# Narrower expert products, an output projection ordered by tile, and a fixed order at the experts' end, in a two-layer hybrid backbone on one core

## The chip, the core and the metric

The kernel runs on one core of a Trainium2 chip. Five engines work beside each other, each with its own instruction stream: TensorE (PE for products, PEld for the loads of its stationary operand), VectorE (DVE), ScalarE (ACT), GpSimd (POOL) and SyncE (SP). A transfer is issued in an engine's stream and carried out by 16 DMA engines. The metric is the device time of one execution in microseconds (us), the median over several runs.

## The reference

The reference is two layers over 256 latent and 256 context tokens of width 1024. Each layer adds a token mixer and then a mixture of experts to its residual stream, both with scales, shifts and gates that come from a conditioning vector.

```
xl = xl + g1_x * (ox @ w_out)                       # output projection
hx = modulate(xl, norm_g[l, 1], sh2_x, sc2_x)       # second norm
pg = softmax(h @ wg + bg); pg_top, g_sel = top_k(pg, 1)
le_g = (h @ we + be) of group g_sel; pe_top, e_sel = top_k(softmax(le_g), 2)
for e in range(16):                                 # D = 1024, d_expert = 512
    y = (silu(h @ w1[e]) * (h @ w3[e])) @ w2[e]
    out = out + combine[:, e:e + 1] * y
xl = xl + g2_x * out
```

Layer 0 mixes with a recurrence (RWKV-7) and a short convolution and carries all 512 tokens on. Layer 1 mixes with differential attention and neighbourhood attention, and only its 256 latent tokens go on to the output. All data is 32-bit.

## The kernel before, in words

**Helpers.** Nearly all products go through `mm` (L214), transposes through `flip` (L219), weight loads through `wload` (L202, on SP's queue). `split` (L224) writes a high part on ACT and the remainder on DVE; a projection is the sum of three products of such parts (`out_mm`: two by L214, the third by L407). `bcast` (L296) reads a modulation row from DRAM into all 128 partitions, on POOL's queue. A planner sets the order of each engine's instructions by dependencies and costs, except where instructions carry a token: those of one token keep the order in which they are written (`inorder`). With `in_line` set all products and transposes carry one.

**Output projection of layer 0** (`out_proj`). The product `wo` has 4 tiles of 128 tokens and two halves h of 512 columns; a tile's half takes 8 input chunks k, 24 products of 512 columns. When a tile's half is complete, DVE multiplies by the gate (`wt`, L435, needs the gate row `g`) and adds to the stream (`x`, L436). `token_norm` follows: sum of squares (L490), scaling with `sc` (L491; `sc` itself is built at L488), and after h = 1 the root and the shift (`hfs`, L502). The **router part** then stands in the same call: per half of the width 4 transposes `rT`, a copy to `hT` on ACT (L514), 4 products `rl` of 20 columns. In h = 1 the order is a table: tiles 0 and 1 whole, then tiles 2 and 3 interleaved by halves of k.

**Experts of layer 0** (`all0`). Each of 16 experts has 96 slots. Its token rows are fetched and transposed (`xt`, copied to `XE`), multiplied by w1 and w3 (`hidden`, four steps q), gated (`middle`), transposed (`gT`) and multiplied by w2 (`down`). In `hidden` the 96 slots are two sets: slots 0 to 63 as stationary operands 64 columns wide, two products side by side (`h`, 32 products of 512 columns per expert), and slots 64 to 95 as operands 32 wide, four side by side (`hc`, 32 products). `down` does the same with `y`, 16 products of each width, for experts 0 to 13; the last two use one operand of 96. The program's order on PE for expert e is fixed: step 0 of e+1, `gT` of e, step 1 of e+1, `down` of e, `xt`, step 2, `xt`, step 3. `middle` stands in the order's gaps on ACT and DVE: `gs` (L893, L894), `gg` (L901, L902, L905). Weights stream in on SP's queue, 12 loads of 512 KB per expert (6.29 MB); 96 token rows of 4 KB come in and as many result rows go out on POOL's (0.79 MB together).

**The experts' end.** The last expert results are not sent through DRAM but placed by products `sc` with 0/1 matrices (`last_two`, two halves per tile, out of one PSUM tag). `fetched` adds the other experts' rows per tile (L940 to L943). Then `tt` (L1083) and `x` (L1084) finish a tile, `norm1_begin` and `norm1_end` normalise it for layer 1, `norm1_turn` transposes it (`nT`), and `proj1` multiplies by `od_w_in`, whose first weights it loads and splits itself (`whi`, `wlo`). After the experts no token is set, so the planner may move this splitting into their end.

Of the kernel before, what the change touches and what calls it, by code (L numbers as in the profile page):

```python
# [11 lines left out]
F32 = mybir.dt.float32  # L12
F32R = mybir.dt.float32r
# [8 lines left out]
P = 128  # L22
# [113 lines left out]
def tile_kernel(ctx: ExitStack, tc: tile.TileContext, I, out, stage=99, dbg=None):  # L136
# [155 lines left out]

    def bcast(pool, tag, l, i, v, bufs=1, n=D, off=0, dst=None):

        t = pool.tile([P, n], F32, tag=tag, name=tag, bufs=bufs) if dst is None else dst
        nc.gpsimd.dma_start(t, bass.AP(tensor=adaD.tensor, offset=adaD.offset + (l * 2 + i) * 6144 + v * D + off,  # L296
                                       ap=[[0, P], [1, n]]))
        return t
# [66 lines left out]

    def norm1_turn(x, khi, klo):

        xn = norm1["xn"]
        xn[0] = cp.tile([P, 2, D], F32, tag="x4", name="xn")
        for t in (2, 3, 0, 1):  # L370
            c = slice(t * 128, t * 128 + 128)
            if t < 2:
                norm1_begin(x, t, lambda inst: None)
                norm1_end(t, lambda inst: None)
            for g in range(2):
                tp = ps("nT", ("ga", "gT")[g])
                for k in range(4):
                    flip(tp[:, k * 128:(k + 1) * 128], token_tile(xn, t)[:, (4 * g + k) * 128:(4 * g + k + 1) * 128],
                         ident)
                split(tp.rearrange("p (k t) -> p k t", k=4), khi[g][:, :, c], klo[g][:, :, c])  # L380
            if t == 3:
                yield xn
        yield

# [13 lines left out]
    def out_gate(l, pool, h):  # L398

        return [bcast(pool, f"g1{i}", l, i, 2, n=512, off=h * 512) for i in range(2 if l == 0 else 1)]  # L400

# [9 lines left out]
    def out_proj(l, Wo, tiles, pool, oT, x1, gate1, done, late, order, tags=("wo",), begun=None):  # L411

        n = len(tiles)
        for h in range(2):
            hs = slice(h * 512, h * 512 + 512)
            g1 = gate1 if h == 0 else out_gate(l, pool, h)
            old, ws = begun if begun and h == 0 else (None, {})
# [9 lines left out]
            for k, a in [(k, a) for k in ks for a in range(n)] if h == 0 else order:  # L429
                out_mm(accs[a], oT, a, k, ws[k], seen[a] == 0, seen[a] == 7)  # L430
                seen[a] += 1
                if seen[a] == 8:
                    t = tiles[a]
                    tt = pool.tile([P, 512], F32, tag="wt", name="wt", bufs=2)
                    inorder(V.tensor_tensor(tt, accs[a], g1[1 if t < 2 else 0], op=ALU.mult), "sums")  # L435
                    (G if h == 0 and a % 2 else V).tensor_tensor(token_tile(x1, t)[:, hs], tt, token_tile(x1, t)[:, hs],  # L436
                                                                 op=ALU.add)
                    if h:
                        done(a, h)
            if h == 0:  # L440
                for a in range(n):
                    done(a, h)


# [5 lines left out]
    def moe(l, tiles, cap, ng, x1, pm, pn, hhi=None, hlo=None):  # L450
# [15 lines left out]
        if l == 0:  # L466
# [7 lines left out]
        ngb = pn.tile([P, D], F32, tag="hT", name="ngb")  # L474
        nc.gpsimd.dma_start(ngb, bass.AP(tensor=I["norm_g"].tensor,
                                         offset=I["norm_g"].offset + (2 * l + 1) * D, ap=[[0, P], [1, D]]))
        sc2 = [bcast(pn, f"sc2{i}", l, i, 4) for i in range(nconds)]
        sh2 = [bcast(pn, f"sh2{i}", l, i, 3) for i in range(nconds)]
        hold = {}

        def token_norm(a, h):
# [22 lines left out]
            if f"h2_{l}" in dbg:  # L504
                nc.sync.dma_start(dbg[f"h2_{l}"][a * P:(a + 1) * P, :], hf)
            acc2 = ps("rl", "rl")
            hT2 = pn.tile([P, D], F32, tag="hT", name="hT")
            for g in range(2):
                acc = ps("rT", "rT")
                for k in range(4):  # L510
                    flip(acc[:, k * 128:(k + 1) * 128],
                                        hf[:, (4 * g + k) * 128:(4 * g + k + 1) * 128], ident)
                hT = hT2[:, g * 512:(g + 1) * 512]
                inorder(act(hT, acc, AF.Copy), "moe")  # L514
                for k in range(4):
                    mm(acc2[:, 0:20], hT[:, k * 128:(k + 1) * 128], wge[:, 4 * g + k, :],
                       start=(g == 0 and k == 0), stop=(g == 1 and k == 3))
            V.tensor_tensor(lg[:, a, :], acc2[:, 0:20], rt[:, 160:180], op=ALU.add)
            if l == 1:
                split(hf, hhi[a], hlo[a])  # L520

# [111 lines left out]
        def experts(pe, ysb, rest, spare=None, next_norm=None):  # L633
# [178 lines left out]
            def all0(rest):  # L812
# [41 lines left out]
                def load(n):  # L854

                    while len(loaded) < min(n, len(stream)):
                        e, u = stream[len(loaded)]
                        q = u % 4
                        if u < 8:
                            w = wload(I[("moe_w1", "moe_w3")[u // 4]][l, e, q * 256:(q + 1) * 256, :], 2, 512)  # L860
                        else:
# [12 lines left out]
                def hidden(e, q):  # L874
# [36 lines left out]
                def down(e, gT):  # L911
# [86 lines left out]
                for e in range(16):  # L998
# [67 lines left out]
                in_line[0] = False  # L1066
                token[0] = None
                slots[:] = base
                turn[0] = 0
# [4 lines left out]
                def last_two(a, t):  # L1074

                    for h in range(2):
                        acc = ps("sc", "h")
                        for i in range(2):
# [680 lines left out]
    with tc.tile_pool(name="pO", bufs=1) as pO:  # L1759

        x1 = [cp.tile([P, 2, D], F32, tag="x", name="x1", bufs=2) for _ in range(2)]
        for i, nm in enumerate(("ctx", "x")):
            nc.gpsimd.dma_start(x1[i], I[nm][0].rearrange("(t p) d -> p t d", p=P))
        gate1 = out_gate(0, pO, 0)
        token[0] = "tail"
# [17 lines left out]
    with tc.tile_pool(name="pe0", bufs=1) as pe:  # L1783
# [7 lines left out]

        experts(pe, ysb, rest, spare, (norm1_scales, norm1_begin, norm1_end))
    es_m.close()
# [33 lines left out]
    with ExitStack() as es:  # L1827
# [3 lines left out]
        dv = pP.tile([P, 4, 512], F32, tag="y", name="dv")  # L1831
        kt = [[pP.tile([P, 4, 512], F32R, tag=t, name=t) for t in tags] for tags in (("rT", "kT"), ("vT", "kkn"))]
        khi, klo = ([t[k // 4][:, k % 4, :] for k in range(8)] for t in kt)
        norm = norm1_turn(x1, *kt)
        with tc.high_priority(offset=150):
            xn = next(norm)
        c1 = pA.tile([P, NC1], F32, name="c1")
        nc.scalar.dma_start(c1, I["cst1"])
        def proj1(c0, n, evac):

            for i in range(4):
                if i % 2 == 0:
                    ws = [wload(Wd[h * 512:(h + 1) * 512, c0 + i * 128:c0 + i * 128 + 256], 4, 256)
                          for h in range(2)]
                whi, wlo = (t.rearrange("p a (k f) -> p (a k) f", f=128) for t in split_tiles())
                for h in range(2):
                    split(ws[h][:, :, (i % 2) * 128:(i % 2 + 1) * 128], whi[:, 4 * h:4 * h + 4, :],
                          wlo[:, 4 * h:4 * h + 4, :])
                acc = ps("pj", "pj")
# [31 lines left out]
        def ev_dq(i, acc):  # L1881
            act(dqT[:, i, :], acc[:, 0:256], AF.Copy)
            rope(dqT[:, i, :])
            if i == 1:
                next(norm)

# [70 lines left out]
    with tc.tile_pool(name="pT", bufs=1) as pT:  # L1957
# [36 lines left out]
        mlo = cp.tile([P, 2, D], F32R, tag="x3", name="mlo")  # L1994
        gate1 = out_gate(1, pT, 0)
        token_norm, route, experts = moe(1, [2, 3], 64, 4, x1, pm, pT, [mhi[:, a, :] for a in range(2)],
# [55 lines left out]
```

## Time and profile before

| what | value |
|---|---|
| median of 3 runs | 1437.96 us (1434.01 to 1445.67) |
| the profiled execution | 1443.12 us, its span 1441.1 us |
| PE busy, share of the span | 1267.0 us, 88% |
| DVE, ACT, POOL busy | 590.1 us (41%), 425.6 us (30%), 218.1 us (15%) |
| mean granted TensorE clock | 0.93 of full |
| moved by DMA | 349.22 MB, mean 242 GB/s |

Times in rows are microseconds from the span's start. Line numbers are those of the kernel before. "<-" in an idle time names what ended it. A busy PE is not PE at its peak, and its granted clock (1.00 is 2.4 GHz, 0.50 is 1.2 GHz) differs by stretch. In this profile layer 0's output projection lies about 460 to 538 us, its experts 557 to 883 us, and layer 1 follows.

### The profile page before, as it was taken

How to read it: one execution, taken by the hardware profiler on the slowest of the kernel's cores; microseconds unless marked ns; L12 is line 12 of the kernel's file. 1: busy time of each engine (PE TensorE's matmuls, PEld its weight loads, DVE VectorE, ACT ScalarE, POOL GpSimd, SP SyncE). 2: the span in 40 equal slices, each digit the busy share in tenths (PEclk: the TensorE clock that was granted, in tenths of full speed). 3: DMA queues.
4: the chain of work that ended last, by engine and by line, in shares of the span. 5: the costliest groups of instructions: out<-in, count | busy, mean ns of one | idle time of the engine just before them, and what ended most of it. 6: DMA issues, size and time to landing. Idle time of an engine off the chain costs nothing. (4 is left out here: it accounts for less than half of the span.)

```text
span 1441.1 us, 22145 instructions
## 1 busy us (share of the span) xinstructions
PE 1267.0 (88%) x8700; PEld 687.0 (48%) x8700; DVE 590.1 (41%) x1329; ACT 425.6 (30%) x835; POOL 218.1 (15%) x271
## 2 busy tenths in 40 slices
PE   5999778888989886999999987799998699999975
PEld 0556556666756672222222223776766544433321
DVE  1326846778656632222112238744636611110003
ACT  2753322222223321221222123324637321111102
POOL 0005520333411301111111120310000100000000
PEclk9999989989999967999999996799999799999998
DMA  9687677766783757999998790651442679999554
GB/s 335 209 256 216 179 181 203 174 172 177 183 262 129 248 221 275 369 383 383 380 382 304 256 365 23 147 139 59 146 169 88 208 265 398 400 396 395 222 223 172
DMA packets 240320, 349.22 MB, mean 242 GB/s; under 512 B 96120, under 2 KB 126104, under 8 KB 239952
## 3 DMA queue, kind: packets, MB, share of 16 engines
q1 hardware_dynamic: 226240, 304.72, 62.9%
q0 software_dynamic: 11264, 34.72, 7.4%
q10 hardware_dynamic: 2704, 8.27, 1.6%
q8 instruction: 72, 1.18, 0.3%
q14 instruction: 40, 0.33, 0.1%
HBM read 326.86 MB, written 20.79 MB: 241 GB/s over the span
## 5 line engine op out<-in xcount | busy, mean ns | idle before, releaser
L214 PE MATMUL y<-w,gT 128*64 128x512 f32 (+2 forms) x736 | 163.0, 612 | 2.1 <-ACT gT L698 1.5
L214 PE MATMUL pj<-hh,whi 128*128 128x512 f32 x432 | 150.1, 429 | 0.6 <-ACT hh L224 0.3
L214 PE MATMUL h<-w,XT 128*64 128x512 f32 x512 | 138.6, 614 | 5.1 <-issue 5.1
L224 DVE TENSOR_TENSOR wlo<-w,whi 128x512 fp32r<-128x512 f32 (+1 forms) x104 | 84.7, 828 | 111.5 <-ACT whi L224 107.4
L214 PE MATMUL h<-w,XE 128*64 128x512 f32 x512 | 125.4, 611 | 3.0 <-ACT XE L790 2.5
L224 ACT ACTIVATE whi<-w 128x512 fp32r<-128x512 f32 (+1 forms) x104 | 69.9, 700 | 155.4 <-DMA w<-in_ev_w_in_dram 73.0
L214 PEld LDWEIGHTS pj<-hh,whi 128*128 128x128 f32 x432 | 83.6, 202 | 32.4 <-issue 9.8
L214 PEld LDWEIGHTS y<-w,gT 128*64 128x64 f32 (+2 forms) x736 | 44.9, 131 | 101.7 <-issue 91.4
L214 PE MATMUL pj<-hh,wlo 128*128 128x512 f32 x216 | 89.9, 418 | 2.1 <-DVE wlo L224 2.0
L214 PE MATMUL ada<-w,sT 128*32 128x512 f32 x384 | 69.0, 639 | 16.9 <-DMA w<-in_ada_w_dram 10.0
L214 PE MATMUL hc<-w,XE 128*32 128x512 f32 x512 | 68.2, 605 | 0.1
L214 PEld LDWEIGHTS h<-w,XT 128*64 128x64 f32 x512 | 36.4, 138 | 63.6 <-issue 57.6
L894 DVE TENSOR_TENSOR ysb<-y,ysb 64x512 f32<-64x512 f32 x14 | 9.7, 695 | 139.1 <-ACT ysb L893 139.1
L214 PEld LDWEIGHTS h<-w,XE 128*64 128x64 f32 x512 | 31.3, 137 | 57.1 <-issue 48.1
L806 DVE SCALAR_TENSOR_TENSOR ylo<-y,sw,yhi 128x512 fp32r<-128x512 f32 x16 | 12.0, 751 | 100.7 <-ACT yhi L805 100.7
L214 PEld LDWEIGHTS pj<-hh,wlo 128*128 128x128 f32 x216 | 43.5, 201 | 17.0 <-DVE wlo L224 4.7
L689 DVE TENSOR_TENSOR gg<-gg,h 64x512 f32<-64x512 f32 x16 | 11.1, 691 | 95.0 <-ACT gg L688 95.0
L2024 POOL TENSOR_TENSOR x<-x,fg 128x512 f32<-128x512 f32 x2 | 2.8, 1378 | 284.9 <-ACT sq L2023 284.9
L1020 POOL DMA_DIRECT2D yD<-ysb x28 | 15.1, 545 | 171.7 <-ACT ysb L1016 171.7
L1016 ACT ACTIVATE ysb<-y 128x512 f32<-128x512 f32 x14 | 8.4, 597 | 99.6 <-PE y L214 99.6
L1316 DVE TENSOR_TENSOR pr<-T,X 128x8 f32<-128x8 f32 (+14 forms) x120 | 35.7, 298 | 4.0 <-DMA X<-xs 0.6
L893 ACT ACTIVATE gs<-hc 64x512 f32<-64x512 f32 x16 | 9.4, 588 | 88.7 <-PE hc L214 88.7
(542 smaller groups left out, 2269.1 us busy)
## 6 DMA issues: line engine op xcount, KB each, us to landing
w<-in_moe_w_dram SPq DMA_DIRECT2D x384, 512.0 KB
w<-in_ada_w_dram SPq DMA_DIRECT2D x96, 512.0 KB
w<-in_ev_w_in_dram SPq DMA_DIRECT2D x27, 512.0 KB
w<-in_od_w_in_dram SPq DMA_DIRECT2D x24, 512.0 KB
sD<-wad SPq DMA_DIRECT2D x16, 256.0 KB
w<-in_ev_w_out_dram SPq DMA_DIRECT2D x8, 512.0 KB
w<-in_od_w_out_dram SPq DMA_DIRECT2D x8, 512.0 KB
yD<-ysb POOLq DMA_DIRECT2D x28, 128.0 KB, 5.3
```

Of the source, the lines that this page charges most:

```text
L214: inst = nc.tensor.matmul(*args, **kw)
L224: for inst in (act(hi, src, AF.Copy), V.tensor_tensor(lo, src, hi.bitcast(F32), op=ALU.subtract)):
L689: V.tensor_tensor(gg[64:128], gg[64:128], acc[64:128], op=ALU.mult)
L806: V.scalar_tensor_tensor(lo, y, w, hi.bitcast(F32), op0=ALU.mult, op1=ALU.subtract))
L893: put(act(o, acc[0:64, :], AF.Copy))
L894: put(V.tensor_tensor(o, acc[64:128, :], o, op=ALU.add))
L1016: put(act(o[:, 0:512], y[0], AF.Copy))
L1020: nc.gpsimd.dma_start(yD[e * cap:e * cap + 64, hs_], o[64 * h:64 * h + 64, 0:512])
L1316: V.tensor_tensor(pr[:, :, 0:t], T[:, 0:t, :].rearrange("p s j -> p j s"), X[:, 0:t, t][:, None, :].to_broadcast([P, 8, t]), op=ALU.mult)
L2024: (V if h else G).tensor_tensor(xt_[:, hs], xt_[:, hs], fg[:, hs], op=ALU.mult)
```

## The change

Three parts, all in or around layer 0's second half.

1. `hidden` and `down` split each 64-wide product into two of 32 columns, four side by side, as `hc` and the narrow `y` were before. The multiplications are the same; products and operand loads of that kind double in number.
2. In `out_proj`, h = 1 goes tile after tile. The router part is returned as a function and called one tile later. In layer 0 the order of PE is fixed from h = 1 on. The gate rows of both halves are read at the start, and the broadcasts of layer 0 (4 gate rows of 256 KB, `ngb`, two `sc` and two `sh` of 512 KB) move from POOL's queue to SP's, under a token with the first expert's weights behind them.
3. The experts' end keeps its token to the last `tt`. `fetched` of the last two tiles and the split of the first `od_w_in` weights are placed behind `gT` of expert 15; the first two loads of those weights are issued there; transposes of tiles 2 and 3 stand between the `last_two` calls, which get PSUM banks of their own.

```
-            g1 = gate1 if h == 0 else out_gate(l, pool, h)
+            g1 = gate1[h]
...
                     if h:
-                        done(a, h)
+                        wait.append(done(a, h))
+                        if len(wait) > 1:
+                            wait.pop(0)()
             if h == 0:
+                in_line[0] = l == 0
                 for a in range(n):
                     done(a, h)
+        wait.pop(0)()
+        in_line[0] = False
...
-        order = [(k, a) for a in range(2) for k in (4, 5, 6, 7, 0, 1, 2, 3)]
-        order += [(k, a) for ks in (range(4, 8), range(4)) for a in (2, 3) for k in ks]
+        order = [(k, a) for a in range(4) for k in (4, 5, 6, 7, 0, 1, 2, 3)]
...
-            mm(A[64 * j:64 * j + 64, :], XTe[e][:, 2 * q + i, ab], w[j][:, i], start=(q + i == 0),
-               stop=(q + i == 4))
+            for b in (0, 32):
+                mm(A[64 * j + b:64 * j + b + 32, :], XTe[e][:, 2 * q + i, b:b + 32], w[j][:, i],
+                   start=(q + i == 0), stop=(q + i == 4))
...
-                                mm(y[0][64 * h:64 * h + 64, :], gT[:, 2 * g + i, ab], ws[i][:, h], start=(g + i == 0),
-                                   stop=(g + i == 2))
+                                for b in (0, 32):
+                                    mm(y[0][64 * h + b:64 * h + b + 32, :], gT[:, 2 * g + i, b:b + 32], ws[i][:, h],
+                                       start=(g + i == 0), stop=(g + i == 2))
...
                     else:
+                        load(len(stream))
+                        slots[:] = base
+                        turn[0] = 0
+                        first = next_norm[3]()
                         for n in (2, 3):
                             fetched(n, put)
+                        first(0)
...
-                begin1, end1 = next_norm[1:]
-                last_two(*order[0])
+                begin1, end1, _, turn1 = next_norm[1:]
+                last_two(*order[0], "hh")
                 begin1(x1, 2, put)
-                last_two(*order[1])
+                last_two(*order[1], ("h", "ps"))
                 end1(2, put)
+                turn1(2)
                 begin1(x1, 3, put)
                 end1(3, put)
-                for n in (2, 3):
-                    last_two(*order[n])
+                turn1(3)
+                first(1)
+                last_two(*order[2], "yy")
+                last_two(*order[3], ("ps", "y"))
+                token[0] = None
```

Here `first_weights` issues the two loads, and the function it returns splits one of the two 128-column parts; `proj1` takes them for its first two steps.

PE in the router stretch of layer 0's output projection, before: a router part (`rT`, `rl`) of one of the first two tiles, in among the `wo` of later tiles.

```order
L407 MATMUL wo<-late_4807,cT 128x512
L214 MATMUL wo<-whi,cT 128x512
L214 MATMUL wo<-wlo,cT 128x512
L407 MATMUL wo<-whi,cT 128x512
L214 MATMUL wo<-whi,cT 128x512
L219 MATMUL rT<-cst,hfs 128x128 x4
L214 MATMUL wo<-wlo,cT 128x512
L219 MATMUL rT<-cst,hfs 128x128 x4
L214 MATMUL rl<-rt,hT 128x20 x4
L407 MATMUL wo<-whi,cT 128x512
L214 MATMUL wo<-late_4807,cT 128x512
L214 MATMUL wo<-late_4808,cT 128x512
```

And with the change, the router part of tile 0 or 1 and the next tile's first products:

```order
L427 MATMUL wo<-whi,o_4782 128x512
L219 MATMUL rT<-cst,hfs 128x128 x4
L214 MATMUL rl<-rt,hT 128x20 x4
L219 MATMUL rT<-cst,hfs 128x128 x4
L214 MATMUL rl<-rt,hT 128x20 x4
L214 MATMUL wo<-whi,cT 128x512
L214 MATMUL wo<-wlo,cT 128x512
L427 MATMUL wo<-whi,cT 128x512
```

Before, the router's transposes and products were laced singly into other tiles' `wo`; now a whole router part stands in one piece between two tiles, and the parts of the last two tiles stand together at the end.

DVE at the end of layer 0's experts, before (`gs` and `gg` are of expert 15, `wlo` the split of layer 1's first weights, `room` the work of `fetched`):

```order
L942 TENSOR_TENSOR room<-room,g2t 128x1024
L224 TENSOR_TENSOR wlo<-w,whi 128x512
L943 TENSOR_TENSOR x_4758<-room,x_4758 128x1024
L894 TENSOR_TENSOR gs<-hc,gs 64x512
L907 SCALAR_TENSOR_TENSOR gg<-gg,sw,h 64x512
L224 TENSOR_TENSOR wlo<-w,whi 128x512
L907 SCALAR_TENSOR_TENSOR gg<-gg,sw,gs 32x512
L941 SCALAR_TENSOR_TENSOR room<-room,wk 128x1024
```

And with the change:

```order
L979 TENSOR_TENSOR x_4758<-room,x_4758 128x1024
L929 TENSOR_TENSOR gs<-hc,gs 64x512
L942 SCALAR_TENSOR_TENSOR gg<-gg,sw,h 64x512
L942 SCALAR_TENSOR_TENSOR gg<-gg,sw,gs 32x512
L977 SCALAR_TENSOR_TENSOR room<-room,wk 128x1024
L978 TENSOR_TENSOR room<-room,g2t 128x1024
L979 TENSOR_TENSOR x_4757<-room,x_4757 128x1024
L977 SCALAR_TENSOR_TENSOR room<-room,wk 128x1024
L978 TENSOR_TENSOR room<-room,g2t 128x1024
L979 TENSOR_TENSOR x_4757<-room,x_4757 128x1024
L224 TENSOR_TENSOR wlo<-w,whi 128x512 x2
```

The two splits, which stood ahead of expert 15's `gs` and between its `gg`, moved behind the last `room` work.

## Rows read from the trace of the kernel before

**Rows 1.** Windows: us, busy of PE, PEld, DVE, ACT, POOL; PEclk, DMA share, GB/s.
```profile
473.00:496.20 23.20, 22.89 (x97) 18.08 (x97) 16.39 (x24) 9.90 (x18) 9.62 (x14) 1.00 1.00 359
501.30:537.70 36.40, 32.54 (x143) 28.32 (x143) 12.12 (x28) 8.81 (x19) 3.21 (x6) 0.69 0.62 231
557.00:858.20 301.20, 299.32 (x1749) 83.50 (x1749) 71.38 (x138) 62.97 (x109) 52.38 (x82) 1.00 0.98 354
...
560.00:780.00 220.00, 219.87 (x1314) 60.64 (x1314) 50.04 (x108) 44.91 (x80) 35.75 (x58) 1.00 1.03 377
```
**Rows 2.** Timeline, one expert: start, us, engine, line, out<-in, count [idle before].
```profile
640.46 0.55 PE L219 MATMUL xt<-cst,xe 96*128 96x96 f32 x4
...
640.94 1.94 PE L214 MATMUL h<-w,XE 128*64 128x512 f32 x8
...
641.42 0.14 PEld L214 LDWEIGHTS h<-w,XE 128*64 128x64 f32 x2 [0.28 <-issue]
641.85 0.14 PEld L214 LDWEIGHTS h<-w,XE 128*64 128x64 f32 x2 [0.28 <-issue]
...
642.80 1.06 PE L214 MATMUL hc<-w,XE 128*32 128x512 f32 x8
643.80 0.55 PE L219 MATMUL xt<-cst,xe 96*128 96x96 f32 x4
...
653.42 5.80 PE L214 MATMUL y<-w,gT 128*64 128x512 f32 x32
...
659.15 0.55 PE L219 MATMUL xt<-cst,xe 96*128 96x96 f32 x4
```
**Rows 3.** The same timeline, from the last `hc` to `gT`.
```profile
646.15 1.07 PE L214 MATMUL hc<-w,XE 128*32 128x512 f32 x8
...
649.34 0.68 DVE L905 TENSOR_TENSOR gg<-gg,gs 32x512 f32<-32x512 f32 x1
...
650.07 0.55 PE L219 MATMUL gT<-cst,gg 96*128 96x96 f32 x4
```
**Rows 4.** Timeline of SP's queue late in the experts.
```profile
772.18 35.75 SPq L202 DMA_DIRECT2D w<-in_moe_w_dram  x8
```
**Rows 5.** Waits of PE, 557 to 858 us: total, times, longest.
```profile
PE h L214 <- DMA w<-in_moe_w_dram: 0.5, 1, 0.5
```
**Rows 6.** Timelines of layer 0's output projection, several engines.
```profile
488.69 0.55 POOL L296 DMA_DIRECT2D g<-adaD  x1
...
496.89 0.69 DVE L435 TENSOR_TENSOR wt<-wo,g 128x512 f32<-128x512 f32 x1 [3.09 <-DMA g<-adaD]
...
501.32 1.11 PE L219 MATMUL rT<-cst,hfs 128*128 128x128 f32 x4 [5.12 <-DVE hfs L502]
```
**Rows 7.** The same stretch of PE, later.
```profile
513.90 1.07 PE L214 MATMUL rl<-rt,hT 128*128 128x20 f32 x8
...
525.73 1.91 PE L219 MATMUL rT<-cst,hfs 128*128 128x128 f32 x8 [2.54 <-DVE hfs L502]
534.12 3.60 PE L214 MATMUL rl<-rt,hT 128*128 128x20 f32 x16
```
**Rows 8.** Timeline of the experts' end, several engines.
```profile
858.77 1.22 DVE L942 TENSOR_TENSOR room<-room,g2t 128x1024 f32<-128x1024 f32 x1
...
864.49 0.63 ACT L224 ACTIVATE whi<-w 128x512 fp32r<-128x512 f32 x1 [4.97 <-DMA w<-in_od_w_in_dram]
...
867.01 0.69 DVE L894 TENSOR_TENSOR gs<-hc,gs 64x512 f32<-64x512 f32 x1
...
869.91 0.90 PE L219 MATMUL gT<-cst,gg 96*128 96x96 f32 x4
...
871.39 10.05 PE L214 MATMUL y<-w,gT 128*96 128x512 f32 x16 [0.58 <-ACT gT L1007]
...
872.54 1.28 DVE L941 SCALAR_TENSOR_TENSOR room<-room,wk 128x1024 f32<-128x1024 f32 x1 [2.69 <-ACT room L940]
...
882.89 0.69 DVE L1083 TENSOR_TENSOR tt<-sc,g2t 128x512 f32<-128x512 f32 x1
```

More of the change, by code (lines that the diff above doesn't have):

```diff
@@ L364, in norm1_end, with norm1_turn, norm1_ctx, first_weights @@
             put(V.scalar_tensor_tensor(n[:, hs], n[:, hs], s, norm1["sh"][i][:, hs], op0=ALU.mult, op1=ALU.add))
[L366 to L383, printed above, removed]
+    def norm1_turn(t):
+        if not norm1.get("kt"):
+            norm1["kt"] = [[pP.tile([P, 4, 512], F32R, tag=tg, name=tg) for tg in tags]
+                           for tags in (("rT", "kT"), ("vT", "kkn"))]
+        khi, klo = norm1["kt"]
+        c = slice(t * 128, t * 128 + 128)
+        for g in range(2):
+            tp = ps("nT", ("ga", "gT")[g])
+            for k in range(4):
+                flip(tp[:, k * 128:(k + 1) * 128],
+                     token_tile(norm1["xn"], t)[:, (4 * g + k) * 128:(4 * g + k + 1) * 128], ident)
+            split(tp.rearrange("p (k t) -> p k t", k=4), khi[g][:, :, c], klo[g][:, :, c])
+    def norm1_ctx(x):
+        norm1["xn"][0] = cp.tile([P, 2, D], F32, tag="x4", name="xn")
+        for t in range(2):
+            norm1_begin(x, t, lambda inst: None)
+            norm1_end(t, lambda inst: None)
+            norm1_turn(t)
+    first_w = {}
+    def first_weights():
+        Wq = I["od_w_in"][0]
+        ws = [wload(Wq[h * 512:(h + 1) * 512, 0:256], 4, 256) for h in range(2)]
+        def make(i):
+            whi, wlo = first_w[i] = [t.rearrange("p a (k f) -> p (a k) f", f=128) for t in split_tiles()]
+            for h in range(2):
+                split(ws[h][:, :, i * 128:(i + 1) * 128], whi[:, 4 * h:4 * h + 4, :], wlo[:, 4 * h:4 * h + 4, :])
+        return make
     def split_tiles():
@@ L398, in out_gate @@
     def out_gate(l, pool, h):
-        return [bcast(pool, f"g1{i}", l, i, 2, n=512, off=h * 512) for i in range(2 if l == 0 else 1)]
+        return [bcast(pool, f"g1{h}{i}", l, i, 2, n=512, off=h * 512, eng=nc.sync if l == 0 else None)
+                for i in range(2 if l == 0 else 1)]
     def out_mm(acc, oT, a, k, w, start, stop):
@@ L411, in out_proj @@
     def out_proj(l, Wo, tiles, pool, oT, x1, gate1, done, late, order, tags=("wo",), begun=None):
-        n = len(tiles)
+        n, wait = len(tiles), []
         for h in range(2):
             hs = slice(h * 512, h * 512 + 512)
-            g1 = gate1 if h == 0 else out_gate(l, pool, h)
+            g1 = gate1[h]
             old, ws = begun if begun and h == 0 else (None, {})
@@ L474, in moe @@
         ngb = pn.tile([P, D], F32, tag="hT", name="ngb")
[L475 to L478, printed above, removed]
+        eng = nc.sync if l == 0 else None
+        inorder((eng or nc.gpsimd).dma_start(ngb, bass.AP(tensor=I["norm_g"].tensor, ap=[[0, P], [1, D]],
+                                                          offset=I["norm_g"].offset + (2 * l + 1) * D)), "loads")
+        sc2 = [bcast(pn, f"sc2{i}", l, i, 4, eng=eng) for i in range(nconds)]
+        sh2 = [bcast(pn, f"sh2{i}", l, i, 3, eng=eng) for i in range(nconds)]
         hold = {}
@@ L505, in token_norm, with logits @@
                 nc.sync.dma_start(dbg[f"h2_{l}"][a * P:(a + 1) * P, :], hf)
[L506 to L520, printed above, removed]
+            def logits():
+                acc2 = ps("rl", "rl")
+                hT2 = pn.tile([P, D], F32, tag="hT", name="hT")
+                for g in range(2):
+                    acc = ps("rT", "rT")
+                    for k in range(4):
+                        flip(acc[:, k * 128:(k + 1) * 128], hf[:, (4 * g + k) * 128:(4 * g + k + 1) * 128], ident)
+                    hT = hT2[:, g * 512:(g + 1) * 512]
+                    inorder(act(hT, acc, AF.Copy), "moe")
+                    for k in range(4):
+                        mm(acc2[:, 0:20], hT[:, k * 128:(k + 1) * 128], wge[:, 4 * g + k, :],
+                           start=(g == 0 and k == 0), stop=(g == 1 and k == 3))
+                V.tensor_tensor(lg[:, a, :], acc2[:, 0:20], rt[:, 160:180], op=ALU.add)
+                if l == 1:
+                    split(hf, hhi[a], hlo[a])
+            return logits
         def route():
@@ L1763, in tile_kernel @@
             nc.gpsimd.dma_start(x1[i], I[nm][0].rearrange("(t p) d -> p t d", p=P))
-        gate1 = out_gate(0, pO, 0)
+        gate1 = [out_gate(0, pO, h) for h in range(2)]
         token[0] = "tail"
@@ L1790, in spare @@
             return (lambda i, h: a[i][:, h]), (lambda i, h: b[:, 2 * i + h]), c.rearrange("p i (a t) -> p i a t", a=4)
[L1792 removed]
+        experts(pe, ysb, rest, spare, (norm1_scales, norm1_begin, norm1_end, first_weights, norm1_turn))
     es_m.close()
@@ L1831, in tile_kernel @@
         dv = pP.tile([P, 4, 512], F32, tag="y", name="dv")
[L1832 to L1836, printed above, removed]
+        khi, klo = ([t[k // 4][:, k % 4, :] for k in range(8)] for t in norm1["kt"])
+        xn = norm1["xn"]
         c1 = pA.tile([P, NC1], F32, name="c1")
@@ L1841, in proj1 @@
             for i in range(4):
-                if i % 2 == 0:
+                if i % 2 == 0 and (c0 or i):
                     ws = [wload(Wd[h * 512:(h + 1) * 512, c0 + i * 128:c0 + i * 128 + 256], 4, 256)
                           for h in range(2)]
[L1845 to L1848, printed above, removed]
+                if c0 or i > 1:
+                    whi, wlo = (t.rearrange("p a (k f) -> p (a k) f", f=128) for t in split_tiles())
+                    for h in range(2):
+                        split(ws[h][:, :, (i % 2) * 128:(i % 2 + 1) * 128], whi[:, 4 * h:4 * h + 4, :],
+                              wlo[:, 4 * h:4 * h + 4, :])
+                else:
+                    whi, wlo = first_w[i]
                 acc = ps("pj", "pj")
@@ L1884, in ev_dq @@
             if i == 1:
-                next(norm)
+                norm1_ctx(x1)
         def ev_dk(i, acc):
@@ L1994, in tile_kernel @@
         mlo = cp.tile([P, 2, D], F32R, tag="x3", name="mlo")
-        gate1 = out_gate(1, pT, 0)
+        gate1 = [out_gate(1, pT, h) for h in range(2)]
         token_norm, route, experts = moe(1, [2, 3], 64, 4, x1, pm, pT, [mhi[:, a, :] for a in range(2)],
```

21 lines of the change are left out of this document (12 added, 9 removed).

## The prediction

> **What bounds the kernel now.** I read the windows first, because the busy share of PE over the whole span averages stages with different limits. In layer 0's experts PE is busy 299.3 of 301.2 us at a granted clock of 1.00 [rows 1]: what shortens PE's own stream there shortens the kernel, as long as weights come in time. The window of the output projection's second half is different: PE is busy 32.5 of 36.4 us, but at a clock of 0.69 [rows 1], and behind a gap of 5.1 us in which it waits for DVE [rows 6]. The third place is the experts' end, where PE waits for a chain through ACT and DVE [rows 8]. Then I read the timeline of one expert to see what its 18.7 us consist of, and the DMA queue for what a shorter period would meet.
>
> **Part 1, products 32 wide.** One expert runs from 640.46 to 659.15, a period of 18.69 us [rows 2]. Products that stand side by side make a round. Two rounds of 64-wide products start 0.43 apart (641.42 and 641.85). Four rounds of them take 642.80 − 640.94 = 1.86 us, which is 0.14 to 0.15 more than 4 × 0.427; two rounds of the 32-wide take 643.80 − 642.80 = 1.00, again 0.15 more than 2 × 0.427 [rows 2]. So I read a round as 0.427 whichever its width and 0.15 as the price of going over to another width. Per expert there are 16 rounds of `h`, 8 of `hc` and 12 of `y`: 36 × 0.427 = 15.37 us. Three groups of transposes with 0.48 each (640.46 to 640.94) make 1.44. The remaining 1.88 us lie on 12 changes (two in each of four steps of `hidden`, four in `down`), 0.157 each.
>
> With the change the rounds are as many, since four 32-wide products fill the place of two 64-wide. All have one width, so only the changes to and from the transposes are left: three stretches, 0.47 us. Period: 15.37 + 1.44 + 0.47 = 17.28 us, 1.41 less. But `gT` needs the gated rows: from the last `hc` group's start to `gT` it was 650.07 − 646.15 = 3.92 us, the last link being a 0.68 us `gg` on DVE [rows 3]. After the change that path is covered by 2 + 6 rounds and an exit, 8 × 0.427 + 0.16 = 3.58, so PE waits 0.34: period 17.62, gain 1.07. Thirteen full periods give 13.9, the start and the last two experts (whose `y` is 96 wide and unchanged) about 1: I take **−15 us**. What is not shown by any row is a long run of 32-wide rounds. The two ends: without the wait −20 (14 × 1.41); and if the whole excess of the narrow pair belongs to its rounds, they cost 0.50, the period is 36 × 0.50 + 1.44 = 19.4 and the part costs +10. I stay with 0.427 because the 64-wide rows show the same 0.15 with twice the rounds, so it goes with the change of width and not with the round.
>
> Operand loads double too. At 641.42 and 641.85 two loads of 64 columns take 0.14 us together while products run, and the rounds are still 0.43 apart [rows 2], so they lie beside the products. The Trainium skill, TensorE: Matmul & The Clock Gate, Part 3 (Packing small matmuls), says on the contrary that a load of the stationary operand overlaps products in flight only when it goes to another row group; all operands here fill all 128 rows, so by that rule the loads would stand bare. By the rows the term is 0, by the rule it is the price of the last rival below.
>
> The weights have to keep pace. An expert takes 6.29 MB of weights and 0.79 MB of rows; at the 377 GB/s of 560 to 780 us [rows 1] that is 18.8 us, more than the new period. It is hidden because loads run far ahead: late in the experts SP's queue stands 35.75 us over 8 loads, because no buffer is free [rows 4], and in the whole stretch PE waited 0.5 us for a weight [rows 5]. A deficit of about 1.2 us per expert over 14 is some 17 us, less than that lead. I cost it at nothing; without the lead it would cost (18.8 − 17.6) × 14 = 17.
>
> **Part 2, the output projection.** The gate row of h = 1 is issued on POOL at 488.69 and DVE waits 3.1 us for it until 496.89; through the norm this leads to `rT` at 501.32 behind 5.1 us of idle PE [rows 6]. Reading it early removes most of that wait; the same 3.5 MB then pass before the first expert's weights, which have slack until 557. After that PE has 48 `wo` products and four router parts (8 `rT`, 16 `rl` each) until the end at 534.12 + 3.60 = 537.72 [rows 7]. A `wo` is 22.89/97 = 0.236 us at full clock [rows 1], 48 are 11.3. A router part at half clock is 2 × 1.11 + 3.60 = 5.8, less some overlap: 5.4 [rows 6, 7]; at full clock its `rl` are 2 × 1.07 [rows 7], and with the ACT copies between it comes to about 4.5 (an estimate from these rows). Counted from the last product before the gap at 496.2 [rows 1], with 1 us of wait left: at full clock 496.2 + 1 + 11.3 + 18 = 526.5, −11; `wo` at full and router at half clock 496.2 + 1 + 11.3 + 21.6 = 530.1, −7.6; all at half clock 496.2 + 1 + 22.6 + 21.6 = 541, +4. The waits for `hfs` of the last tiles (2.5 us at 525.73 [rows 7]) go since the router part comes one tile later. I take **−8**: the sparse router part leaves PE thinly used, as in the rows where the clock was 0.69, while dense `wo` ran at 1.00. What follows until the first expert product at 557 is the routing on DVE and is unchanged. Layer 1's projection keeps its planner and gets a one-tile shift of the same kind: 0.
>
> **Part 3, the experts' end.** Now ACT splits a weight of layer 1 at 864.49, after 4.97 us of waiting for its load, and DVE's `gs` of expert 15 comes only at 867.01, `gT` at 869.91, `y` at 871.39 [rows 8]. With the split behind, DVE goes from `room` (858.77 + 1.22) through one more 1.2 us `x` into `gs` at about 861.3, and `gT` at 863.5: 6.4 us earlier. The work of `fetched` follows `gT` as before at +2.6 (872.54 against 869.91), six operations of some 1.25 us, then two splits and the two of `y`, 0.69 each: `tt` at 863.5 + 2.6 + 7.5 + 2.8 = 876.4 against 882.89, −6.5. What the splitting then no longer takes from layer 1's start, about −1.5, goes on top: **−8**. Ends: −3, if the transposes of tiles 2 and 3, now in line, hold up the placing products; −11, if `y` also runs at full clock (16 × 0.427 = 6.9 instead of 10.05 [rows 2, 8]).
>
> **Sum.** −15 − 8 − 8 = −31 us against the profiled execution's 1443.1, so 1412. The median of the runs shown, 1438.0, lies 5.1 below that execution; I subtract it too: **1407 us**, −2.2%. I call a change "the same" within 1%, 14 us, about what a measurement of this kernel can tell.
>
> **Rivals.**
> *The output projection gives its gain back* (clock or waits in line: fixed order means a router part that waits for `hfs` holds all `wo` behind it). For it: clock 0.69 in that stretch [rows 1]. Against: the wait for the gate row surely goes. Part 2 is worth −2, the sum −25: 1413.
> *Rounds of 32 wide are dearer.* If half the excess of the narrow pair is theirs, a round is 0.463 and the period 16.7 + 1.4 + 0.3 = 18.4: −4 from part 1, sum −20: 1418. With all of it, +10 and a sum of −6: 1432, no change. Against: equal excess in the 64-wide rows.
> *The weights become the bound.* If the lead of the loads is used up, the period is that of the queue, 18.8, and part 1 is worth nothing: sum −16, 1422. Against: the 35.75 us at a standstill [rows 4].
> *Slower: bare operand loads.* The reorder of loads beside products may fail with four operands per round. Then each round costs its loads, 0.14 more, the price of two loads in rows 2: 36 × 0.14 − 1.41 = 3.6 us per expert, +51 over 14, against −16 from the other parts: +35, 1473. It decides from (31 + 14)/(14 × 36) = 0.09 us per round on. Against: the loads of 64 and 32 columns that lie hidden now.
>
> **Chances.** The forecast 0.58; the projection's gain lost 0.17; dearer rounds 0.12, of which the half 0.07 and the whole 0.05; the weights 0.07; bare loads 0.06. The boundary for faster is 1423.6. The first two, the half-dear rounds and half of the weights' case lie below it, 0.86; some of that is taken for two of them together: faster 0.83, the same 0.11, slower 0.06. The range from 1394 to 1425 takes in the full clock and no wait at `gT` below (part sums −20 − 11 − 11, 1396), and the first three rivals above; it leaves out the whole-dear rounds and the bare loads.
>
> **What would show it.** The period of an expert (`xt` to `xt`): 17.6 right, 17.3 without the wait, over 18.3 dearer rounds or weights; a wait of PE for a weight tells these two apart. An idle time of PE in front of `gT` of about 0.3 shows the path through `gg`. `rT` of the first tile should follow the last `wo` within 1 to 2 us, and the last `rl` end 8 us sooner counted from the window's start, the granted clock telling which of the two prices holds. `gT` of the last expert should come about 5 us after its `hc`, and `tt` 13 us after. I would be wrong above all if 32-wide rounds in a long row start more than 0.43 us apart.

## The result, and the profile after

The changed kernel takes 1422.4 us (median of 4 runs, 1420.5 to 1422.6) against 1440.0 of the kernel before (4 runs, 1434.0 to 1445.7): a ratio of 0.9865 with the interval [0.9828, 0.9902], 17.6 us faster by the medians. The forecast was 1407 us with a range from 1394 to 1425. Sign and range held; the gain is little more than half of the 31 us forecast.

Totals hide where that comes from, so I cut the program at four events on PE. **A** ends where the 48 products `wo<-wc,o` start; **P** goes from there to the first expert product `h`; **E** to the end of the last `hc`; **end** to the first `pj` of layer 1; **rest** is what follows. In microseconds, from the one profiled execution of each kernel (the kernels below the changed one are the experiments of the next section):

| kernel | A | P | E | end | rest | P+E+end | median |
|---|---|---|---|---|---|---|---|
| before | 473.3 | 83.7 | 301.2 | 42.7 | 540.2 | 427.6 | 1440.0 |
| changed | 476.0 | 84.9 | 287.2 | 34.8 | 537.9 | 406.9 | 1422.4 |
| part 1 alone | 475.1 | 83.1 | 291.4 | 37.4 | 540.2 | 411.9 | 1426.2 |
| part 3 alone | 475.2 | 82.1 | 302.5 | 33.0 | 535.1 | 417.6 | 1429.9 (one run) |
| rows ahead, no fixed order | 465.4 | 79.8 | 287.4 | 36.0 | 538.1 | 403.3 | 1409.7 |
| fixed order, rows as before | 474.4 | 86.0 | 286.9 | 35.6 | 543.2 | 408.4 | 1424.4 |
| laced | 469.5 | 70.8 | 286.8 | 35.4 | 537.8 | 393.0 | 1404.1 |
| transposes first | 469.3 | 77.0 | 285.2 | 35.5 | 540.4 | 397.7 | 1409.2 (one run) |
| filled | 471.5 | 81.2 | 286.2 | 35.7 | 541.2 | 403.0 | 1417.4 (one run) |
| hidden narrow | 469.7 | 84.7 | 294.2 | 35.4 | 539.9 | 414.3 | 1425.7 (one run) |
| late gT | 477.0 | 84.8 | 281.9 | 36.0 | 544.9 | 402.7 | 1426.3 (one run) |
| laced, later gT, additions on GpSimd | 469.0 | 70.7 | 282.2 | 37.2 | 540.3 | 390.1 | 1401.5 |
| laced, later gT | 477.0 | 70.9 | 281.1 | 35.6 | 539.9 | 387.5 | 1405.4 |

On the compute engines A carries the same instructions in the same order in all these kernels (on SP the gate rows take the place of expert weights in its last 2 us where they are read early), and still it lies between 465 and 477 us, which is as much as some of the effects asked for. The mean granted clock of A is 0.92 in the three kernels in which it is longest and 0.93 or 0.94 in the others; no run tests whether that is the cause. A kernel's total therefore carries several microseconds that are not its own, and verdicts below rest on the three stretches in the middle. These are single executions too. Where kernels have the same instructions in a stretch, P agrees within 0.2 us for the output projection of the change (84.7 to 84.9) and within 1.6 for that of before (82.1 to 83.7), E within about 2.

E, where part 1 acts, is 14.1 shorter (forecast −15), the experts' end 7.8 (forecast −8), but the output projection's P grew by 1.2 where −8 was forecast. The windows of its router stretch are the first thing to read: us, busy of PE, PEld, DVE, ACT, POOL, then granted clock, DMA share, GB/s. The first is from the first `rT` to the last `rl`, the others the `wo` of tiles 2 and 3 inside it.

```profile
500.60:541.90 41.30, 34.25 (x144) 28.16 (x144) 12.51 (x28) 8.70 (x19) 3.25 (x6) 0.68 0.58 211
507.00:515.10 8.10, 8.10 (x26) 6.44 (x26) 2.58 (x7) 0.20 (x1) 0.55 (x1) 0.67 0.16 65
520.10:528.40 8.30, 8.30 (x25) 6.54 (x26) 1.67 (x4) 0.00 (x0) 0.54 (x1) 0.65 0.89 287
```

A tile's 24 products take 8.1 and 8.3 us, not the 5.6 of full clock: they run at 0.50 for their first 5 us and more (to 512.3 and to 525.9 us) and then at 1.00. The whole stretch has the clock 0.68, as before ([rows 1]: 0.69), but is 41.3 us long instead of 36.4. What is thin in it shows in the timeline of PE:

```profile
500.60 0.66 PE L219 MATMUL rT<-cst,hfs 128*128 128x128 f32 x4 [1.98 <-DVE hfs L529]
501.94 1.84 PE L214 MATMUL rl<-rt,hT 128*128 128x20 f32 x8 [0.69 <-ACT hT L542]
...
534.71 1.09 PE L219 MATMUL rT<-cst,hfs 128*128 128x128 f32 x4 [1.42 <-DVE hfs L529]
```

```profile
PE rl L214 <- ACT hT L542: 5.6, 8, 0.7
```

DVE no longer waits for the gate row, and PE's wait at the first `rT` is down from 5.1 us ([rows 6]) to 2.0. New is the wait in front of every `rl`: its copy `hT` is made from the transposes just ahead of it, and nothing stands between. There are eight of them, 5.6 us (the last line: total, times, longest).

In the experts, one period, and two groups of operand loads of the `y` ahead of it, answer to [rows 2, 3]:

```profile
636.25 0.13 PEld L214 LDWEIGHTS y<-w,gT 128*32 128x32 f32 x4 [0.30 <-issue]
636.68 0.13 PEld L214 LDWEIGHTS y<-w,gT 128*32 128x32 f32 x4 [0.30 <-issue]
...
641.09 0.55 PE L219 MATMUL xt<-cst,xe 96*128 96x96 f32 x4
...
650.40 0.55 PE L219 MATMUL gT<-cst,gg 96*128 96x96 f32 x4 [0.29 <-DVE gg L940]
...
652.62 1.04 PE L214 MATMUL hc<-w,XE 128*32 128x512 f32 x8
...
653.48 5.33 PE L214 MATMUL y<-w,gT 128*32 128x512 f32 x48
...
658.75 0.55 PE L219 MATMUL xt<-cst,xe 96*128 96x96 f32 x4
```

The period is 658.75 − 641.09 = 17.66 us (18.69 before), with rounds 0.43 apart and a wait of 0.29 in front of `gT`. Over the experts the waits of PE are these (total, times, longest):

```profile
PE gT L219 <- DVE gg L940: 3.5, 11, 0.4
...
PE h L214 <- DMA w<-in_moe_w_dram: 0.6, 1, 0.6
```

At the end, the rows that answer to [rows 8]:

```profile
853.56 0.90 PE L219 MATMUL gT<-cst,gg 96*128 96x96 f32 x4
855.04 9.76 PE L214 MATMUL y<-w,gT 128*96 128x512 f32 x16 [0.58 <-ACT gT L1043]
...
863.63 1.28 DVE L224 TENSOR_TENSOR wlo<-w,whi 128x512 fp32r<-128x512 f32 x2
...
866.49 0.69 DVE L1121 TENSOR_TENSOR tt<-sc,g2t 128x512 f32<-128x512 f32 x1 [0.34 <-PE sc L214]
```

Before, `gT` started 11.7 us after the end of the last `hc` (858.2, where E ends) and now 5.6 (848.0); `tt` follows `gT` by 12.9 us, 13.0 before. `y` is still slow (9.8 us).

### The profile page after: what moved, and what is told of

It is laid out like the page before. It is cut to its first block, busy times and chain, and to the rows that moved or that the text cites. A ratio compares the mean times of both kernels' runs of the same rounds, so it can differ in the third digit from the quotient of the medians.

```text
span 1420.8 us, 23611 instructions
## 1 busy us (share of the span) xinstructions
PE 1248.2 (88%) x9436; PEld 691.0 (49%) x9436; DVE 592.6 (42%) x1329; ACT 425.2 (30%) x835; POOL 215.3 (15%) x262
## 3 DMA queue, kind: packets, MB, share of 16 engines
q8 instruction: 78, 1.28, 0.4%
## 5 line engine op out<-in xcount | busy, mean ns | idle before, releaser
L214 PE MATMUL y<-w,gT 128*32 128x512 f32 (+2 forms) x960 | 156.2, 601 | 2.1 <-ACT gT L728 1.5
L214 PE MATMUL h<-w,XE 128*32 128x512 f32 x1024 | 124.5, 604 | 3.1 <-ACT XE L820 2.5
L214 PEld LDWEIGHTS y<-w,gT 128*32 128x32 f32 (+2 forms) x960 | 48.7, 120 | 89.3 <-issue 75.7
L214 PEld LDWEIGHTS h<-w,XE 128*32 128x32 f32 x1024 | 28.1, 110 | 56.2 <-issue 47.2
L1358 DVE TENSOR_TENSOR pr<-T,X 128x8 f32<-128x8 f32 (+14 forms) x120 | 35.6, 297 | 3.7 <-DMA X<-xs 0.3
L214 PEld LDWEIGHTS hc<-w,XE 128*32 128x32 f32 x512 | 16.1, 111 | 40.3 <-issue 30.9
```

Source lines behind the costliest of these rows:

```text
L214: inst = nc.tensor.matmul(*args, **kw)
L1358: V.tensor_tensor(pr[:, :, 0:t], T[:, 0:t, :].rearrange("p s j -> p j s"), X[:, 0:t, t][:, None, :].to_broadcast([P, 8, t]), op=ALU.mult)
```

## The experiments

My theory after the result: the early rows gained what they should; the fixed order lost more than that, because each router part now stands as a thin piece in which PE waits for `hT`, and the clock that falls there slows the dense `wo` behind it. The rival: the early rows gained nothing, or the clock falls whatever the order.

**Part 1 alone.** The kernel before with the two loops over `b` and nothing else.

> The kernel before with part 1 alone (products 32 wide). I compare two stretches: P, from the start of the 48 gate-free products wo<-wc,o to the first expert product h (83.7 us before, 84.9 with the whole change), and E, from the first expert product h to the start of the sc products behind the last hc (301.2 before, 287.1 with the whole change). Theory (part 1 pays in the experts alone): E 287 to 288, P 83.7, end of the experts to the first pj as before (42.7). Rival (the three parts need each other, a shorter experts' stretch meets the weights): E above 292 and a wait of PE for weights of over 2 us. Time about 0.990 of before.

Ratio 0.9890 [0.9838, 0.9942]. P 83.1 as it was, no wait for weights. E came out at 291.4, not 287 to 288, and the end at 37.4 instead of 42.7. Late in E, PE waits 3.8 us for a copy of `gT` on ACT, which it does not do in the changed kernel; what held ACT there is not shown. From `h` to `pj`, which takes in both stretches, it is 328.8 against 343.9, −15.1, the forecast term.

**Rows ahead.** The router part is called at once and the planner orders PE; gate rows and broadcasts stay early.

```
-                        wait.append(done(a, h))
-                        if len(wait) > 1:
-                            wait.pop(0)()
+                        if l == 0:
+                            done(a, h)()
+                            continue
...
-                in_line[0] = l == 0
...
-        order = [(k, a) for a in range(4) for k in (4, 5, 6, 7, 0, 1, 2, 3)]
+        order = [(k, a) for a in range(2) for k in (4, 5, 6, 7, 0, 1, 2, 3)]
+        order += [(k, a) for ks in (range(4, 8), range(4)) for a in (2, 3) for k in ks]
```

> The changed kernel with the gate rows and broadcasts early on SP, but the router part called at once and the order of PE in the output projection left to the planner, as before. Theory (the early rows gain about 3 us, the router part in one piece in a fixed order loses about 4 to 5): P about 80, 4 to 5 us shorter than with the whole change, and total 4 us shorter. Rival (the early rows gain nothing, since the norm of the first tile is late for another reason): P 83 to 84.

P 79.8: the early rows are worth 2.3 to 3.9 us against the three kernels whose output projection is that of before (82.1 to 83.7). With the planner's order `rl` waits for `hT` nowhere. Ratio 0.9778 [0.9707, 0.9849]; by the medians it is 12.7 us shorter than the whole change, where 4 were expected, but A alone differs by 10.6 between the two profiled executions.

**Fixed order.** The other half: gate rows and broadcasts back on POOL's queue, `g1 = gate1[h] or out_gate(l, pool, h)`, the order as in the change.

> The changed kernel with the fixed order and the router part one tile later, but gate rows and broadcasts on POOL's queue as before, those of the second half late. Theory (early rows gain 3, fixed order loses 4 to 5): P about 88, 3 us longer than with the whole change. Rival (the fixed order loses nothing, the early rows cost something by holding back the first expert's weights): P at or below 84.

P 86.0, 2.3 to 3.9 more than in those three kernels and 1.1 more than with the whole change; 88 was expected. Both signs are as the theory has them, but the parts may not add: in the planner's order the early rows save 2.3 to 3.9, in the fixed order 1.1. `rT` still waits 4.1 us once and `rl` 5.6 in all.

**Laced.** The router part becomes a generator of four steps (transposes of half 0, of half 1, `rl` of half 0, of half 1); those of tiles 0 and 1 are taken one step at a time between the chunks of tiles 2 and 3.

```
+                if h and l == 0 and a > 1 and seen[a] in (3, 4, 6, 7):
+                    next(wait[a - 2])
```

> The changed kernel with the router parts of tiles 0 and 1 laced into the wo products of tiles 2 and 3 in the fixed order (transposes of both halves after chunks 3 and 4 of a tile, the products rl after chunks 6 and 7), those of tiles 2 and 3 with both transposes first. Theory (the fixed order lost by PE's waits for the copy hT, 8 times 0.69 us, and by the half clock that they bring): waits of rl for hT fall from 8 to 2 or less, the wo of tiles 2 and 3 run at full clock (0.24 us each), P 72 to 76, total 9 to 12 us shorter than with the whole change. Rival (the clock falls whatever the order, since the router products are short): P 80 to 84, granted clock below 0.8 in the stretch from the first rT to the last rl.

P 70.8, below the expected 72 to 76: −14.1 against the change with the same products. Ratio 0.9750 [0.9668, 0.9832]. In the window of the laced `wo` the granted clock is full, and of the waits of `rl` and `rT` there remain one short one and that for the last tile's norm.

```profile
494.00:510.00 16.00, 15.82 (x96) 13.25 (x95) 9.67 (x22) 4.50 (x11) 2.69 (x5) 1.00 0.60 219
```

The waits of PE in P (total, times, longest):

```profile
PE rT L219 <- DVE hfs L534: 4.0, 1, 4.0
...
PE rl L214 <- ACT hT L546: 0.3, 1, 0.3
```

The rival, that the clock falls whatever the order, is out. Two runs part the waits from the clock.

**Transposes first.** Still in one piece between tiles; only the loops over the halves are split, as in the laced kernel but without the steps.

> The changed kernel; in each router part the transposes of both halves stand first and then all products rl, still in one piece between two tiles. Theory (waits and clock together): the second half's copy is hidden, so rl waits for hT 4 times instead of 8, about 2.8 us less, and little of the clock comes back, since the piece stays thin: P 80 to 83 (84.9 with the change, 70.8 laced). Rival (the waits alone matter, the clock follows them): P below 78.

P 77.0, 7.9 shorter: the rival's forecast (below 78) came true, not mine. I had the waits wrong (2 with 0.6 us in all remained, not 4), and more of the clock came back with them than I thought: the 24 `wo` of tile 3 run at full clock, those of tile 2 still do not. The timeline of one piece, and then the windows of the two tiles' `wo`, columns as above:

```profile
505.99 1.03 PE L219 MATMUL rT<-cst,hfs 128*128 128x128 f32 x8
507.33 1.96 PE L214 MATMUL rl<-rt,hT 128*128 128x20 f32 x16 [0.31 <-ACT hT L541]
```

```profile
498.80:506.00 7.20, 7.20 (x26) 5.66 (x26) 2.58 (x7) 0.20 (x1) 0.55 (x1) 0.76 0.19 74
509.20:514.80 5.60, 5.60 (x25) 4.49 (x25) 2.58 (x7) 0.20 (x1) 0.54 (x1) 1.00 0.93 263
```

**Filled.** The order of the change; in front of each group of `rl` three products that nobody reads.

```
+                    for _ in range(3):
+                        mm(spare_, oT[0][0][:, 0:128], ws[7][0], start=True, stop=True)
```

> The changed kernel with 24 products more: in each router part, behind each half's transposes, three products of 512 columns into a PSUM bank that nothing reads stand in PE's order where it waited 0.69 us for hT. They take away no wait of the chain and remove no work. Theory (half of the fixed order's loss is the clock that the thin pieces bring): the granted clock in the stretch from the first rT to the last rl rises from 0.68 to above 0.85, the wo of tiles 2 and 3 take 5.6 us each instead of 7.9 and 8.2, P 76 to 80 although PE has more to do. Rival (the clock has nothing to do with it): P 85 to 90.

P 81.2: 24 products more and 3.7 us less. The clock of the stretch rose from 0.68 to 0.78 and tile 3's `wo` took 5.6 us instead of 8.3; I expected 0.85 and 76 to 80, and missed since the first and the last piece, which stand behind idle waits for `hfs`, stayed at half clock, and behind the first piece the start of tile 2's `wo` as well (7.5 us, mean clock 0.73). The windows of the stretch and of the `wo` of tiles 2 and 3:

```profile
496.10:534.10 38.00, 36.19 (x168) 30.12 (x168) 12.55 (x29) 8.70 (x19) 3.23 (x6) 0.78 0.58 215
503.00:510.50 7.50, 7.50 (x25) 5.93 (x26) 2.58 (x7) 0.20 (x1) 0.55 (x1) 0.73 0.18 70
515.00:520.60 5.60, 5.60 (x26) 4.55 (x26) 1.66 (x4) 0.00 (x0) 0.54 (x1) 1.00 0.83 295
```

Nothing but the density of PE's work was changed here, so this part of the loss is the clock. How the other 10 us between this kernel and the laced one divide into waits and clock is not shown.

**Hidden narrow.** The changed kernel with `down` in its two widths as before.

> The changed kernel with the product by w2 in its two widths as before, the products by w1 and w3 32 wide. Theory (the saving is in changes of width, 0.157 us each; this brings back four per expert): a period of 18.2 us instead of 17.6 and E about 296 (287.2 with the change). Rival (64-wide rounds are dearer than 32-wide ones; a third of them come back): period 18.07, E about 293.8. Rounds of y should start 0.427 apart in both widths.

E 294.2, by itself nearer to the rival's 293.8 than to 296; but E of kernels with the same experts differs by 2 us (285.2 to 287.4), so E does not decide. The timeline does: the period is 654.85 − 636.61 = 18.24 us (18.2 by the theory, 18.07 by the rival), and rounds of the 64-wide `y` start 0.43 apart (631.36 and 631.79), as 32-wide ones do (636.25 and 636.68 in the changed kernel). `y` takes 636.61 − 630.88 = 5.73 us, exactly the 5.73 of [rows 2], and the last `hc` 0.97 in front of it; in the changed kernel, all 32-wide, `y` takes 658.75 − 653.48 = 5.27 and that `hc` 0.86. So `hc` and `y` are 0.57 longer with four changes of width more, 0.14 each. The 0.157 that I had worked out holds within a tenth.

```profile
629.91 1.04 PE L214 MATMUL hc<-w,XE 128*32 128x512 f32 x8
630.88 5.80 PE L214 MATMUL y<-w,gT 128*64 128x512 f32 x32
631.36 0.14 PEld L214 LDWEIGHTS y<-w,gT 128*64 128x64 f32 x2 [0.28 <-issue]
631.79 0.14 PEld L214 LDWEIGHTS y<-w,gT 128*64 128x64 f32 x2 [0.29 <-issue]
636.61 0.55 PE L219 MATMUL xt<-cst,xe 96*128 96x96 f32 x4
...
654.85 0.55 PE L219 MATMUL xt<-cst,xe 96*128 96x96 f32 x4
```

**Late gT.** For experts 0 to 13 the transposes `gT` go behind the products `h` of the next expert's step 1 (`hidden(e + 1, 1, turn_gate)`, called between `h` and `hc`).

> The changed kernel with the transposes gT moved behind the products h of the next expert's step 1, in front of its hc (for experts 0 to 13). Theory (PE's 0.34 us in front of gT is the only price of the shorter period): the waits of PE for gg go from 3.5 us in 11 to under 0.5, no new wait of y for the copy gT, E 283 to 284 instead of 287.2. Rival (y then waits for the copy of gT, 0.5 us and its signalling): E 287 or more.

E 281.9, a little below the 283 to 284 expected; the wait for `gg` in front of these `gT` is gone, and `y` does not wait. In the timeline the period is 658.29 − 640.99 = 17.30, the 17.28 worked out for no wait at all.

```profile
640.99 0.55 PE L219 MATMUL xt<-cst,xe 96*128 96x96 f32 x4
...
651.67 0.55 PE L219 MATMUL gT<-cst,gg 96*128 96x96 f32 x4
...
658.29 0.55 PE L219 MATMUL xt<-cst,xe 96*128 96x96 f32 x4
```

**Part 3 alone.** Products in their two widths, layer 0's output projection as before.

> The kernel before with part 3 alone in layer 0 (products in their two widths, output projection of layer 0 as before). Measured from the first expert product h to the first pj of layer 1: 343.9 us before, 328.8 with part 1 alone, 322.0 with the whole change. Theory (part 3 is worth what the whole change has over part 1 alone, 6.8, and does not depend on part 1): 336 to 338. Rival (part 1 and part 3 shorten the same wait at the end): 341 or more.

From `h` to `pj` 335.5, −8.4, a little more than the 336 to 338 expected. Parts 1 and 3 alone sum to −23.5, together they give −21.9: nearly independent.

**All together, additions on GpSimd.** Laced, late gT, and `G.tensor_tensor` for the last line of `fetched`.

> The changed kernel with the laced router parts, gT behind the products h of step 1, and the four additions x of fetched (1.22 us each on DVE) given to GpSimd. Theory (three independent stretches): P 70 to 71.5; E 282 to 284; from the last hc to the first pj 31 to 32 us instead of 34.8, since DVE is the bound there and loses 2.4 us ahead of gs and 2.4 behind; total, stretches alone, 1394 against 1420.8 of the changed kernel's profile, less or more by where the stretch ahead of P falls (465 to 477 us so far). Rival (an addition on GpSimd takes 2.6 us or more and the next tt waits for it): last hc to first pj 35 or more.

P 70.7, E 282.2 as expected, but the end 37.2, longer than the 35.4 of the laced kernel: here the rival was right. Ratio 0.9723 [0.9686, 0.9759]. The rows of DVE and POOL show why:

```profile
819.64 1.22 DVE L989 TENSOR_TENSOR room<-room,g2t 128x1024 f32<-128x1024 f32 x1
820.78 1.28 DVE L988 SCALAR_TENSOR_TENSOR room<-room,wk 128x1024 f32<-128x1024 f32 x1
820.95 3.38 POOL L990 TENSOR_TENSOR x<-room,x 128x1024 f32<-128x1024 f32 x1 [9.05 <-DVE room L989]
822.09 3.32 DVE L989 TENSOR_TENSOR room<-room,g2t 128x1024 f32<-128x1024 f32 x1
825.49 2.35 POOL L990 TENSOR_TENSOR x<-room,x 128x1024 f32<-128x1024 f32 x1 [1.16 <-DVE room L989]
826.17 0.74 DVE L953 SCALAR_TENSOR_TENSOR gg<-gg,sw,h 64x512 f32<-64x512 f32 x1
826.94 1.45 DVE L953 SCALAR_TENSOR_TENSOR gg<-gg,sw,gs 32x512 f32<-32x512 f32 x1
```

The same product on DVE takes 1.22 us alone and 3.32 beside GpSimd's addition. Of the four additions two lengthen such a product (by 2.1 and 2.0 us), one the two `wlo` (3.44 instead of 1.28) and one a `gg` (1.45 instead of 0.74). That is 7.0 us in all, against the 4.9 of the four additions that left DVE.

**Laced, later gT, additions on DVE.**

> The changed kernel with the laced router parts and the later gT, all additions of fetched back on DVE. Theory (GpSimd's additions were the only thing that made the experts' end longer, since DVE's operations beside them took 3.3 us instead of 1.2): P 70 to 71.5, E 281 to 284, last hc to first pj 35 to 36 as in the laced kernel, the sum of the three 387 to 391 (390.1 with the additions on GpSimd, 406.9 with the change, 427.6 before). Rival (the later gT lengthens the end): last hc to first pj 37 or more.

P 70.9, E 281.1, end 35.6, sum 387.5: as expected, 40.0 us shorter than before and 19.3 shorter than the change. Ratio 0.9750 [0.9725, 0.9776], median 1405.4; its A, at 477.0, is among the longest. Which of the last two kernels is faster in total stays open: the stretches speak for this one by 2.6 us, the medians for the other by 3.9. Both beat the change and the kernel before.

## Why the prediction was half right

**Part 1** held step by step: rounds 0.43 apart in the long 32-wide rows, period 17.66 (17.62 forecast), a wait of 0.3 to 0.4 in front of `gT` (0.34), weights never late by more than 0.6. That the excess of 0.15 goes with a change of width was shown by the hidden-narrow run (0.14 for each change, with the 64-wide and the 32-wide rounds alike). Operand loads, now four per round with 0.13 us together, cost nothing that shows, since the rounds stay 0.43 apart. The rule of the Trainium skill, TensorE: Matmul & The Clock Gate, Part 3, by which they would have stood bare, does not agree with these rows. The Trainium skill, TensorEngine Tiling (Array Packing), Key Properties, says that changing the tiling mode drains TensorE; the hidden-narrow run puts 0.14 us on a change of width.

**Part 3** held too: `gT` came 5.6 us behind the last `hc` (about 5 forecast), `tt` 12.9 us behind that (13), and −8.4 us for the part alone.

**Part 2** failed, by 9.2 us. The step was "`wo` at full and router at half clock 496.2 + 1 + 11.3 + 21.6". Read from the rows of after, the same sum from the end of tile 1's `wo` (498.6) to the last `rl` (541.9) is waits 3.4, `wo` 16.3, router parts 23.5. So the term for `wo` was mis-sized most (+5.0): I took the dense products at full clock because they ran at 1.00 ahead of the stretch, though each tile's 24 now stand right behind a thin piece and begin at 0.50; over the two windows their clock is 0.67 and 0.65. The router parts (+1.9) I had priced from a row in which the transposes of both halves precede all `rl` [rows 7], so that the copy of one half is hidden behind the other; the order of the change, four `rT`, four `rl`, four `rT`, four `rl`, shows the copy bare; the order rows ahead of the prediction have it. The waits for `hfs` (+2.4) did not all go, the last tile's cannot. This is the first rival, which I gave 0.17, and it went further than its −2. The range held because it had been drawn to take this rival in. The early rows did what I said (`rT` 24.6 us behind the start of P instead of 28.0), and the 1 to 2 us of wait that were forecast at the first `rT` were there.

A and rest moved by +2.7 and −2.3, less than they differ between kernels with the same instructions there (A 465 to 477; rest 537.9 to 544.9 with the whole change). What varies them between executions was not tried. Between the two profiled executions the program is 20.3 us shorter, 10.7 short of the 31; 9.2 of that are part 2, 1.1 parts 1 and 3 together, 0.4 A and rest.

## What to carry to other kernels

A fixed order of PE is only as good as what stands between a producer and its consumer: put a short dependent chain (transposes, copy, small products) into the gaps of dense work instead of between two blocks of it, which here was worth 14 us with the same instructions. When a sum takes a duration from a row, check that the new order keeps what hid the waits in that row, and allow for the lower clock in dense work behind a thin piece, which here began at 0.50. Before work is moved to an idle engine, look whether the busy one slows beside it.

## What the runs showed of the hardware

Adding 24 products that nobody reads shortened P by 3.7 us, with the granted clock of the router stretch up from 0.68 to 0.78.

Rounds of products side by side start 0.43 us apart whether they are two of 64 columns or four of 32, and going over from one width to the other costs 0.14 us each time.

Operations of GpSimd and VectorE with two operands from SBUF did not run beside each other: DVE's 1.22 us became 3.32. GpSimd's addition began at 820.95 while a DVE operation ran to 822.06, and ended at 824.33; the DVE product that started at 822.09 ended 1.08 us after that. Beside the next addition (825.49 to 827.84) the `gg` with an operand in PSUM (`h`) took its usual 0.74 us. This looks like one waiting for the other in turn, which is what the Trainium skill, SBUF — State Buffer, "SBUF: two separate sides", says of the port pair that the two share: whoever starts first holds it for the whole instruction.
